# Chunked attention in a two-layer encoder: where the low half of k, the last round and five small layer-norm columns stand in the order of the work

## The chip, the cores and the metric

The program runs on one core of one Trainium2 chip. The time is the device time of one execution in microseconds; the kernel before was run three times with a median of 1211.73 us (1211.3 to 1212.54). All records of a profile come from one further execution.

## The reference, cut to what matters

Two layers act on a sequence of 512 frames with 1024 features. Layer 0 mixes with a gated linear attention, layer 1 with a softmax attention of 16 heads of 64 features in chunks of 64 frames; with eight chunks to the left, a frame sees every earlier chunk and its own. Each mixer and each squared-ReLU MLP is followed by a layer norm of `alpha*x + (1+gate)*y`, and shift, scale and gate come from a conditioning vector. The change lies in layer 1:

```
q, k, v = split(u @ w_in + b_in, 3)
s = einsum('bhtd,bhjd->bhtj', q / 8, k) + bias[h, clip(t - j)]
p = softmax(s over the keys j)
o = einsum('bhtj,bhjd->bhtd', p, v) @ w_out
x = layer_norm(alpha * x + (1 + g1) * o, ln_g, ln_b)
u = x * (1 + sc2) + sh2
```

## The kernel before, in words

Everything is held transposed: features on the 128 partitions, the 512 frames along the free dimension. A float32 product is made of three matmuls on a high and a low part of each operand (`mm3`); "hi" is a rounded copy made on ACT, "lo" the rest, made on DVE. The wrappers `V`, `A`, `G` and `T` keep each compute engine's instructions in the order in which the Python code emits them, so the order of the calls is the order of DVE, ACT, POOL and PE. (All of them carry line 47 in the profile, that of the wrapper.) DMAs are issued on SP and wait there for a free buffer.

`att` (from line 971) computes layer 1's attention in rounds `p = -1..5` (line 1091). A round makes the q and the k tile of the head pair `p + 2` and the scores of the heads `2p + 2` and `2p + 3`, and multiplies the probabilities of the heads `2p` and `2p + 1` with v:

- `mtile` multiplies one weight tile with u (24 matmuls); `evac_qk` copies the result with its bias to a tile `f` on ACT and gives back two functions: `hi` (casts of 64 rows on ACT: two for k, four for q) and `lo` (two subtractions of 64x512 on DVE). These are called `q_hi`, `q_lo`, `k_hi`, `k_lo`.
- `s_mm(h)` (line 992) makes the scores of head h, keys on partitions, in four blocks of 512, 384, 256 and 128 queries.
- `s_a(h)` (line 1006) adds the bias of each block on DVE (four `SCALAR_TENSOR_TENSOR` of ps and ng), lets ACT copy the part further than 256 from the diagonal, takes the maximum over the blocks on DVE and ends with `partition_all_reduce` on POOL, which gives the maximum over all keys, tile `mb`.
- `s_b1(h)` (line 1031) subtracts `mb` from the four blocks on DVE; `s_b2(h)` (line 1039) takes the exponential in two ACT instructions.
- `pv(h)` multiplies with v; a block of ones beside v gives the denominators. `fin1(p)` copies these on ACT and takes Ln and Exp for a first reciprocal, `fin2(p)` refines it and multiplies on DVE (four instructions), `fin3(p)` adds v's bias and splits into hi and lo.

In the rounds up to `p = 4`, DVE has the order fin2, s_b1 (odd head), fin3, s_a (even head), q_lo, s_a (odd head), s_b1 (even head), k_lo. ACT has s_b2 of the even head last, and then fin1 of the next round. The last round, `p = 5`, has an order of its own: q_hi and q_lo directly behind s_mm(12), k's evacuation ahead of s_a(12), k_lo between s_a(12) and s_a(13), and the subtraction and exponential of head 12 are left to `t1` (line 1146), which stands in the list `ev` (line 1179) of the work between attention and layer norm. There `t1`, `t2`, `t3`, `t5` finish the heads 12 to 15, mixed with the matmuls of the output projection that `boundary` makes.

`boundary` (line 330) makes the output projection, the layer norm and the next layer's input; for the attention it is called with `late=True`. Its first statement is `lnc = mk_cols()`: `ln_cols` (line 307) makes four 128x8 column constants from `ln_g`, `ln_b` and the shift and scale columns, in three `tensor_tensor` and two `tensor_scalar` on DVE. So these five stand in DVE's order directly behind the last round and ahead of `t1`. Behind `t5`, `fill` splits weights of the output projection (`wlo`, on DVE) and of the next MLP (`fhi`, `flo`).

`fill(2)` in the rounds issues the DMAs of weights until two tiles are at hand. Those of the attention's q and k and of the first four output tiles are read already split, so they cost neither DVE nor ACT anything.

Of the kernel before, what the change touches and what calls it, by code (L numbers as in the profile page):

```python
# [35 lines left out]
SH1, SC1, G1, SH2, SC2, G2 = range(6)  # L36
# [23 lines left out]
def trunk(ctx, tc, xT, c, ada, cols, gk1, gk2, w_qk, w_v, w_g, w_go, a_qk, a_v, a_tab,  # L60
# [19 lines left out]
    def bank():  # L80
        return psp.tile([P, S], F32, tag="ps", name=nm("ps"))
# [137 lines left out]
    def fill(n=None):  # L219
        n = state["look"] if n is None else n  # L220
        while len(ready_w) < n and state["pos"] < len(plan):
            emit_unit()
# [77 lines left out]
    def mtile(u, f=True):  # L300
        w = next_w(f)
        ps = bank()
        for k in range(KT):
            mm3(ps, wk(w, k), uk(u, k), k == 0, k == KT - 1)
        return ps

    def ln_cols(l, i, nxt):
        r = {}
        g = col[:, C_LNG + (l * 2 + i) * 8:C_LNG + (l * 2 + i) * 8 + 8]
        b = col[:, C_LNB + (l * 2 + i) * 8:C_LNB + (l * 2 + i) * 8 + 8]  # L310
        r["g"], r["b"] = g, b
        if nxt is not None:
            nl, sh, sc = nxt
            mS = mods[:, nl, sc * 8:sc * 8 + 8]
            mH = mods[:, nl, sh * 8:sh * 8 + 8]
            a1 = const.tile([P, 8], F32, name=nm("a1"))
            b1 = const.tile([P, 8], F32, name=nm("b1"))
            tt(V, a1, g, mS, ALU.mult)
            tt(V, b1, b, mS, ALU.mult)
            tt(V, b1, b1, mH, ALU.add)  # L320
            ag = const.tile([P, 8], F32, name=nm("ag"))
            ab = const.tile([P, 8], F32, name=nm("ab"))
            V.tensor_scalar(out=ag, in0=g, scalar1=ALPHA, scalar2=None, op0=ALU.mult)
            V.tensor_scalar(out=ab, in0=b, scalar1=ALPHA, scalar2=None, op0=ALU.mult)
            r.update(a=a1, b1=b1, ag=ag, ab=ab)
        return r
# [593 lines left out]
    def evac_qk(p, is_k, ps, h0=0, h1=S):  # L920
        hs = slice(h0, h1)
        rows = slice(0, 64), slice(64, 128)
        f = cur["tmp"].tile([P, S], F32, tag="h32", bufs=2, name=nm("f"))[:, hs]
        b, sc = (col[:, C_BK + p:C_BK + p + 1], 1.0) if is_k else (bq8[:, p:p + 1], 0.125)
        A.activation(out=f, in_=ps, func=AF.Identity, scale=sc, bias=b)
        if h0 == 0:
            (ks if is_k else qs)[p] = act_r()
            if not is_k:
                ql[p] = act_r()
                for i, r in enumerate(rows):  # L930
                    G.memset(ql[p][rows[1 - i], i, :].bitcast(F32), 0.0)
        t = (ks if is_k else qs)[p]

        def hi():
            for i, r in enumerate(rows):
                A.copy(out=t[r, i, hs], in_=f[r, :])
                if not is_k:
                    A.copy(out=t[rows[1 - i], i, hs], in_=f[r, :])

        def lo():  # L940
            for i, r in enumerate(rows):
                o = t[rows[1 - i], i, hs] if is_k else ql[p][r, i, hs]
                lo_of(V, o, f[r, :], t[r, i, hs])
        return hi, lo
# [26 lines left out]
    def att(u, es):  # L971
# [20 lines left out]
        def s_mm(h):  # L992
            p = h // 2
            q, k = qs[p], ks[p]
            pss = [bank()[:, 0:S], bank()[:, 0:384]]
            pl = bank()
            pss += [pl[:, 0:256], pl[:, 256:S]]
            for j in range(4):
                ps = pss[j]
                n = max(W[j], 256)  # L1000
                js = slice(j * P, (j + 1) * P)
                T.matmul(ps[:, 0:n], k[:, h % 2, js], q[:, h % 2, S - n:S], start=True, stop=False)
                T.matmul(ps[:, 0:n], k[:, h % 2, js], ql[p][:, h % 2, S - n:S], start=False, stop=True)
            sps[h] = pss

        def s_a(h):
            sA, sB, b = sab[h]
            sAf = sA.rearrange("p a b -> p (a b)")
            s = [sAf[:, 0:S], sAf[:, S:S + 384], sB[:, 0, 0:256], sAf[:, S + 384:2 * S]]
            for j in range(4):  # L1010
                ps = sps[h][j]
                off = max(W[j], 256) - W[j]
                nb = min(W[j], 256)
                stt(s[j][:, 0:nb], ps[:, off:off + nb], ng[:, h:h + 1], b[:, 0:nb], ALU.add, ALU.add)
                if W[j] > 256:
                    A.copy(out=s[j][:, 256:W[j]], in_=ps[:, 256:W[j]])
            mx = sB[:, 1, :]
            A.copy(out=mx[:, 0:P], in_=s[0][:, 0:P])
            tt(V, mx[:, P:S], s[0][:, P:S], s[1], ALU.max)
            tt(V, mx[:, 256:S], mx[:, 256:S], s[2], ALU.max)  # L1020
            tt(V, mx[:, 384:S], mx[:, 384:S], s[3], ALU.max)
            mb = ab_.tile([P, S], F32, tag="mb", name=nm("mb"))
            G.partition_all_reduce(mb, mx, P, bass_isa.ReduceOp.max)
            st[h] = (s, sAf)
            mbs[h] = mb
# [5 lines left out]
        def s_b1(h):  # L1031
            s, sAf = st[h]
            mb = mbs[h]
            tt(V, s[0], s[0], mb, ALU.subtract)
            tt(V, s[1], s[1], mb[:, P:S], ALU.subtract)
            tt(V, s[2], s[2], mb[:, 256:S], ALU.subtract)
            tt(V, s[3], s[3], mb[:, 384:S], ALU.subtract)

        def s_b2(h):
            s, sAf = st[h]  # L1040
            A.activation(out=sAf, in_=sAf, func=AF.Exp)
            A.activation(out=s[2], in_=s[2], func=AF.Exp)
# [10 lines left out]
        o = []  # L1053
# [37 lines left out]
        for p in range(-1, 6):  # L1091
            pq = mtile(u, False)
            s_pre(2 * p + 2)
            s_pre(2 * p + 3)
            if prev:
                fin1(*prev)
                fin2(p - 1)
            if p >= 0:
                s_b1(2 * p + 1)
            s_mm(2 * p + 2)  # L1100
            q_hi, q_lo = evac_qk(p + 2, 0, pq)
            if p == 5:
                q_hi()
                q_lo()
                fill(2)
            if prev:
                fin3(p - 1)
            if p < 5:
                s_a(2 * p + 2)
                if p >= 0:  # L1110
                    s_b2(2 * p + 1)
                fill(2)
                q_hi()
                q_lo()
                pk = mtile(u, False)
                s_mm(2 * p + 3)
                k_hi, k_lo = evac_qk(p + 2, 1, pk)
                s_a(2 * p + 3)
                k_hi()
                s_b1(2 * p + 2)  # L1120
                k_lo()
                fill(2)
                s_b2(2 * p + 2)
            else:
                pk = mtile(u, False)
                k_hi, k_lo = evac_qk(p + 2, 1, pk)
                s_b2(2 * p + 1)
                k_hi()
                s_a(2 * p + 2)
                k_lo()  # L1130
                s_mm(2 * p + 3)
                s_a(2 * p + 3)
                fill(2)
            if p >= 0:
                prev = (p, pv(2 * p), pv(2 * p + 1))
        s_pre(14)
# [8 lines left out]

        def t1():
            s_mm(14)
            s_b1(12)
            s_a(14)
            s_b2(12)  # L1150
            fill(2)
            s_b(13)

# [19 lines left out]
        def t5():  # L1173
# [3 lines left out]
            fin3(7)  # L1177

        ev = [t1, (0, range(5)), t2, (1, range(3)), e_pv(12), (1, range(3, 5)), e_pv(13), t3, (2, range(3)), t4, e_pv(14), (2, (3, 4)), e_pv(15), t5,
              (0, (5,)), (1, (5,)), (2, (5,)), (3, range(6)), (0, (6,)), (1, (6,)), (2, (6,)), (3, (6,)),  # L1180
              (0, (7,)), (1, (7,)), (2, (7,)), "shift", (3, (7,))]
# [36 lines left out]
    def opener(es, n):  # L1218
        def f():
            if es is not None:  # L1220
                es.close()
            e = ExitStack()
            cur["es"] = e
            cur["tmp"] = e.enter_context(tc.tile_pool(name=f"lnt{n}", bufs=1))
            return cur["tmp"]
        return f
# [4 lines left out]
    o, ev, es = gla()  # L1231
    evac_h, run = mlp_fns()
    u = boundary(o, 0, G1, opener(es, 0), lambda: ln_cols(0, 0, (0, SH2, SC2)), evac_h, ev)
    hs = run(u, 0)
    u = boundary(hs, 0, G2, open_v, lambda: ln_cols(0, 1, (1, SH1, SC1)), None, vfill=vfill)
    cur["es"].close()
    o, ev, es = att(u, cur["es_v"])
    evac_h, run = mlp_fns()
    u = boundary(o, 1, G1, opener(es, 1), lambda: ln_cols(1, 0, (1, SH2, SC2)), evac_h, ev, late=True)
    hs = run(u, 1)  # L1240
    boundary(hs, 1, G2, same, lambda: ln_cols(1, 1, None), None, final=True)
    cur["es"].close()
# [52 lines left out]
```

## Time and profile before

| what | value |
|---|---|
| median of 3 runs | 1211.73 us (1211.3 to 1212.54) |
| the profiled execution's own time | 1211.67 us |
| its span, first to last instruction | 1209.8 us |
| mean granted TensorE clock | 0.994 |
| busy PE / DVE / ACT / POOL | 1177.0 / 827.5 / 555.0 / 49.1 us |
| the attention's rounds and tail in the span | about 640 to 805 us |

The profiled execution stands 0.06 us below the median; 1.87 us lie outside its span. Engines: PE multiplies, DVE and ACT do the elementwise work, POOL the reductions over partitions, SP issues DMAs. A row of the timeline gives start, duration, engine, line, operation, output and input, form and count, and in brackets how long the engine had been idle before and which engine's result ended that.

### The profile page before, as it was taken

Reading aid. Unit: us, or ns where it says so; the run is one execution under the profiler, and the core shown is the slowest. Engines: PE = TensorE matmul, PEld = TensorE weight load, DVE = VectorE, ACT = ScalarE, POOL = GpSimd, SP = SyncE. Lnnn points to the kernel's source line nnn. Section 1 sums busy time; section 2 is a strip of 40 time slices with the busy share of each in tenths; the row PEclk is TensorE's granted clock in tenths of the full one; section 3 lists DMA queues with packets and bytes.
Section 4 is the critical chain, followed back from the end, with each engine's and each line's share of the span. In section 5 each row is a group of like instructions: output and inputs, shape, how many; then the busy total and the mean of one; then the engine's idle time right before and its main releaser. Section 6 shows DMA issues by size and latency. Waiting matters only on the chain.

```text
span 1209.8 us, 15107 instructions
## 1 busy us (share of the span) xinstructions
PE 1177.0 (97%) x5742; PEld 981.0 (81%) x5742; DVE 827.5 (68%) x1359; ACT 555.0 (46%) x870; POOL 49.1 (4%) x61
## 2 busy tenths in 40 slices
PE   9999999999999999999999999998999999999995
PEld 5888888888888888888888777677988888888885
DVE  6788589877676676658835878988874443443467
ACT  4565555484243342343636656564742322422324
POOL 2000000000000000000011313200000000000000
PEclk9999999999999999999999999998999999999998
DMA  9756524028889889844125340330264232332302
GB/s 347 255 184 219 186 105 161 32 88 315 306 306 339 293 305 338 297 143 157 51 104 212 123 150 34 131 115 26 68 206 144 87 105 90 103 105 87 103 2 70
DMA packets 58283, 196.34 MB, mean 162 GB/s; under 512 B 6561, under 2 KB 10913, under 8 KB 58210
## 3 DMA queue, kind: packets, MB, share of 16 engines
q1 hardware_dynamic: 58210, 195.37, 46.7%
q8 instruction: 45, 0.74, 0.2%
q14 instruction: 28, 0.23, 0.1%
HBM read 174.37 MB, written 20.97 MB: 161 GB/s over the span
## 4 chain that ended last, share of the span: by engine, by line
PE 77%; DVE 15%; ACT 6%; issue 2%; DMA 0%; DVEq 0%; ACTq 0%
PE ps L47 76%; DVE af L47 6%; DVE x L47 4%; ACT af L47 3%; ACT ar L47 1%; DVE wlo L47 1%; DVE ar L47 1%; PE warm L47 1%; ACT u L47 1%; DVE d L47 1%; DVE flo L47 1%; DVE t L47 0%; DVE y L47 0%; DVE raw L47 0%; DMA raw<-f 0%
## 5 line engine op out<-in xcount | busy, mean ns | idle before, releaser
L47 PE MATMUL ps<-ar,whi 128*128 128x512 f32 (+1 forms) x2880 | 818.4, 372 | 0.2 <-DVE ar L47 0.2
L47 PEld LDWEIGHTS ps<-ar,whi 128*128 128x128 f32 x2880 | 524.4, 189 | 95.3 <-issue 2.4
L47 PE MATMUL ps<-ar,wlo 128*128 128x512 f32 (+1 forms) x1440 | 524.8, 371 | 0.1
L47 PEld LDWEIGHTS ps<-ar,wlo 128*128 128x128 f32 x1440 | 271.8, 189 | 47.0 <-DVE wlo L47 0.8
L47 ACT CAST whi<-raw 128x1024 fp32r<-128x1024 f32 (+1 forms) x169 | 169.6, 1012 | 202.5 <-PE ps L47 156.2
L47 DVE TENSOR_TENSOR wlo<-raw,whi 128x1024 fp32r<-128x1024 f32 x162 | 197.2, 1223 | 23.3 <-ACT whi L47 21.2
L47 DVE SCALAR_TENSOR_TENSOR x<-ps,mods,x 128x512 f32<-128x512 f32 (+1 forms) x96 | 63.2, 660 | 120.2 <-PE ps L47 119.8
L47 DVE TENSOR_TENSOR h<-r 128x512 f32<-128x512 f32 (+1 forms) x72 | 45.2, 633 | 79.1 <-ACT r L47 78.2
L47 ACT ACTIVATE r<-ps 128x512 f32<-128x512 f32 (+1 forms) x72 | 39.1, 548 | 126.5 <-PE ps L47 126.5
L47 DVE SCALAR_TENSOR_TENSOR raw<-raw,csil 128x1024 f32<-128x1024 f32 x80 | 96.8, 1218 | 0.0
L47 DVE TENSOR_TENSOR ar<-h,ar 128x512 fp32r<-128x512 f32 (+1 forms) x72 | 45.6, 633 | 39.6 <-ACT ar L47 38.5
L47 PE MATMUL ps<-ar,fhi 128*128 128x256 f32 (+1 forms) x320 | 69.0, 310 | 3.7 <-DVE ar L47 2.8
L47 ACT CAST ar<-h 128x512 fp32r<-128x512 f32 (+1 forms) x72 | 41.3, 573 | 50.4 <-DVE h L47 50.4
L47 PE MATMUL ps<-whi,ar 128*128 128x512 f32 x192 | 60.7, 390 | 0.0
L47 PEld LDWEIGHTS ps<-ar,fhi 128*128 128x128 f32 x320 | 52.0, 191 | 8.1 <-DVE ar L47 4.4
L47 PE MATMUL ps<-ar,flo 128*128 128x256 f32 (+1 forms) x160 | 48.8, 305 | 0.0
L47 ACT ACTIVATE af<-x 128x256 f32<-128x256 f32 (+1 forms) x48 | 23.0, 486 | 45.4 <-DVE x L47 42.2
L47 PEld LDWEIGHTS ps<-whi,ar 128*128 128x128 f32 x192 | 36.1, 188 | 7.6
L47 ACT ACTIVATE af<-af 128x1024 f32<-128x1024 f32 (+2 forms) x48 | 32.0, 698 | 20.9 <-DVE af L47 20.4
L47 ACT CAST fhi<-raw 128x1024 fp32r<-128x1024 f32 x30 | 31.2, 1050 | 21.6 <-DMA raw<-a_qk 13.0
L47 ACT ACTIVATE ar<-x,b,a 128x256 fp32r<-128x256 f32 x48 | 28.6, 595 | 25.8 <-DVE x L47 25.8
L47 PE MATMUL ps<-af,vt 128*128 128x512 f32 (+3 forms) x128 | 36.9, 436 | 2.0 <-ACT af L47 2.0
(141 smaller groups left out, 1024.8 us busy)
## 6 DMA issues: line engine op xcount, KB each, us to landing
raw<-f SPq DMA_DIRECT2D x128, 512.0 KB, 4.4
raw<-ada SPq DMA_DIRECT2D x80, 512.0 KB, 4.7
hraw<-ada SPq DMA_DIRECT2D x16, 512.0 KB, 9.0
raw<-a_qk SPq DMA_DIRECT2D x16, 512.0 KB, 5.6
khi_q<-fhi SPq DMA_DIRECT2D x14, 512.0 KB, 3.0
klo_q<-flo SPq DMA_DIRECT2D x14, 512.0 KB, 5.3
whi<-khi_q SPq DMA_DIRECT2D x14, 512.0 KB, 3.2
wlo<-klo_q SPq DMA_DIRECT2D x14, 512.0 KB, 4.4
```

Source lines behind the costliest of these rows:

```text
L47: r = f(*a, **k)
```

## The change

Three things are reordered. No arithmetic is added or removed.

1. In the rounds up to `p = 4`, `k_lo` stands ahead of `s_b1` of the even head instead of behind it.
2. The round `p = 5` takes the order of the others, but with `k_hi` and `k_lo` ahead of `s_a(13)`. `s_b1(12)` and `s_b2(12)` move from `t1` to the end of the round.
3. `ln_cols` of the layer norm behind the attention is called ahead of `att` instead of at the start of that `boundary`.

```diff
@@ -1099,38 +1099,28 @@
                 s_b1(2 * p + 1)
             s_mm(2 * p + 2)
             q_hi, q_lo = evac_qk(p + 2, 0, pq)
-            if p == 5:
-                q_hi()
-                q_lo()
-                fill(2)
             if prev:
                 fin3(p - 1)
-            if p < 5:
-                s_a(2 * p + 2)
-                if p >= 0:
-                    s_b2(2 * p + 1)
-                fill(2)
-                q_hi()
-                q_lo()
-                pk = mtile(u, False)
-                s_mm(2 * p + 3)
-                k_hi, k_lo = evac_qk(p + 2, 1, pk)
+            s_a(2 * p + 2)
+            if p >= 0:
+                s_b2(2 * p + 1)
+            fill(2)
+            q_hi()
+            q_lo()
+            pk = mtile(u, False)
+            s_mm(2 * p + 3)
+            k_hi, k_lo = evac_qk(p + 2, 1, pk)
+            if p == 5:
+                k_hi()
+                k_lo()
+                s_a(2 * p + 3)
+            else:
                 s_a(2 * p + 3)
                 k_hi()
-                s_b1(2 * p + 2)
                 k_lo()
-                fill(2)
-                s_b2(2 * p + 2)
-            else:
-                pk = mtile(u, False)
-                k_hi, k_lo = evac_qk(p + 2, 1, pk)
-                s_b2(2 * p + 1)
-                k_hi()
-                s_a(2 * p + 2)
-                k_lo()
-                s_mm(2 * p + 3)
-                s_a(2 * p + 3)
-                fill(2)
+            s_b1(2 * p + 2)
+            fill(2)
+            s_b2(2 * p + 2)
             if p >= 0:
                 prev = (p, pv(2 * p), pv(2 * p + 1))
...
             s_mm(14)
-            s_b1(12)
             s_a(14)
-            s_b2(12)
             fill(2)
             s_b(13)
...
     cur["es"].close()
+    lnc1 = ln_cols(1, 0, (1, SH2, SC2))
     o, ev, es = att(u, cur["es_v"])
     evac_h, run = mlp_fns()
-    u = boundary(o, 1, G1, opener(es, 1), lambda: ln_cols(1, 0, (1, SH2, SC2)), evac_h, ev, late=True)
+    u = boundary(o, 1, G1, opener(es, 1), lambda: lnc1, evac_h, ev, late=True)
```

## Rows read from the trace of the kernel before

**Rows 1.** The page: span, and busy time of PE and DVE.
```profile
span 1209.8 us, 15107 instructions
...
PE 1177.0 (97%) x5742; PEld 981.0 (81%) x5742; DVE 827.5 (68%) x1359; ACT 555.0 (46%) x870; POOL 49.1 (4%) x61
```
**Rows 2.** Windows: rounds 1 and 4, last round, tail, until the statistics; columns in line one.
```profile
core 0: us, PE busy (x) PEld busy (x) DVE busy (x) ACT busy (x) POOL busy (x), PEclk, DMA share, GB/s
678.24:698.12 19.88, 19.88 (x91) 15.92 (x90) 16.44 (x31) 12.37 (x24) 4.91 (x4) 1.00 0.33 120
...
737.86:757.73 19.87, 18.41 (x82) 14.19 (x81) 16.43 (x32) 12.18 (x24) 4.90 (x4) 1.00 0.12 40
757.73:775.26 17.53, 15.43 (x68) 11.64 (x66) 16.96 (x37) 8.65 (x17) 3.95 (x2) 1.00 0.52 165
775.26:804.82 29.56, 25.95 (x106) 18.80 (x106) 26.85 (x45) 19.91 (x33) 4.11 (x2) 1.00 0.22 72
804.82:828.46 23.64, 18.05 (x133) 16.89 (x133) 20.95 (x33) 8.55 (x13) 0.00 (x0) 0.94 0.40 134
```
**Rows 3.** Timeline of DVE in round p = 4.
```profile
740.83 1.70 DVE L47 TENSOR_TENSOR af<-af,mb 128x512 f32<-128x512 f32 x4
...
746.40 2.10 DVE L47 TENSOR_TENSOR ar<-f,ar 64x512 fp32r<-64x512 f32 x2 [0.40 <-ACT ar L47]
748.52 1.53 DVE L47 SCALAR_TENSOR_TENSOR af<-ps,ng,af 128x256 f32<-128x256 f32 x4
...
751.22 2.53 DVE L47 TENSOR_TENSOR af<-af,mb 128x512 f32<-128x512 f32 x4
753.79 1.40 DVE L47 TENSOR_TENSOR ar<-f,ar 64x512 fp32r<-64x512 f32 x2
757.73 0.69 DVE L47 TENSOR_TENSOR af<-af 128x512 f32<-128x512 f32 x1 [2.54 <-ACT af L47]
```
**Rows 4.** Timeline of ACT in the same round.
```profile
748.30 0.69 ACT L47 ACTIVATE f<-ps,col 128x512 f32<-128x512 f32 x1
...
749.80 1.26 ACT L47 CAST ar<-f 64x512 fp32r<-64x512 f32 x2
753.79 1.36 ACT L47 ACTIVATE af<-af 128x1024 f32<-128x1024 f32 x2 [2.73 <-DVE af L47]
```
**Rows 5.** Who waited for whom on DVE, 674 to 800 us: total, times, longest.
```profile
DVE af L47 <- ACT af L47: 14.7, 7, 2.5
```
**Rows 6.** Timeline of POOL in the same round.
```profile
746.19 1.78 POOL L47 PARTITION_ALL_REDUCE mb<-af  x1 [11.36 <-DVE af L47]
751.47 2.08 POOL L47 PARTITION_ALL_REDUCE mb<-af  x1 [3.50 <-DVE af L47]
```
**Rows 7.** Timeline of DVE from the last round's end into the tail.
```profile
772.20 0.16 DVE L47 TENSOR_TENSOR a<-col,mods 128x8 f32<-128x8 f32 x1
...
772.47 1.04 DVE L47 TENSOR_TENSOR b<-b,mods 128x8 f32<-128x8 f32 x1
...
773.58 1.68 DVE L47 TENSOR_TENSOR af<-af,mb 128x512 f32<-128x512 f32 x4
...
776.62 1.00 DVE L47 TENSOR_TENSOR af<-af 128x384 f32<-128x384 f32 x2
...
782.32 1.02 DVE L47 TENSOR_TENSOR af<-af 128x384 f32<-128x384 f32 x2 [0.48 <-ACT af L47]
```
**Rows 8.** The chain of waits behind the tail: start, us, what.
```profile
800.66 3.51 DVE wlo L47 x3
804.18 4.23 DMA raw<-f
```
**Rows 9.** Timeline of PE at the tail's end and at the layer norm.
```profile
804.87 0.50 PE L47 MATMUL ps<-ar,fhi 128*128 128x512 f32 x1 [1.59 <-DVE ar L47]
...
828.46 2.08 PE L47 MATMUL ps<-af,ones_c 128*128 128x256 f32 x4 [5.54 <-DVE af L47]
```
**Rows 10.** Who waited for whom, 640 to 805 us: total, times, longest.
```profile
PE ps L47 <- DVE ar L47: 4.8, 4, 1.6
```

## The prediction

> **What bounds the kernel now.** I read the page first. PE is busy for 1177.0 of 1209.8 us and DVE for 827.5 [rows 1], so over the whole span PE is the bound; but the change touches the attention alone, and what it is worth must be read there.
>
> Second, the windows by round, each from one fin2 to the next. Round 1 is 19.88 us long with PE never idle; round 4 is 19.87 us long with PE idle for 1.46 [rows 2]. A round that keeps its length when PE gets idle time is not paced by PE: in the early rounds PE works off a backlog, later it waits.
>
> Third, DVE and ACT in round 4. DVE is busy without a break but for two waits: 0.40 us ahead of q_lo and 2.54 us ahead of fin2 [rows 3]. ACT waits 2.73 us for s_b1 of the even head, takes its exponential as soon as that ends (753.79), then does fin1, and fin2 starts when fin1 is done (757.73) [rows 3, 4]. That closes a loop: s_b1 ends, exponential and fin1 on ACT, fin2, s_b1 (odd), fin3, s_a, q_lo, s_a, s_b1 (even), and again. From s_b1's end (751.22 + 2.53 = 753.75) to fin2 are 3.98 us. **k_lo lies in them**: 753.79 to 755.19, while DVE could not have gone on with fin2 anyway [rows 3]. It costs the loop nothing today.
>
> Fourth, how many rounds are so. In 674 to 800 us DVE waited for ACT 7 times, 14.7 us in total, 2.5 at the longest [rows 5]. Five waits of 2.54 are 12.7; the rest are two in the tail, one of 0.48 at 782.32 [rows 7] and one of about 1.5. So the loop paces the five transitions into the rounds 1 to 5.
>
> Fifth, behind the rounds. From 775.26 to 804.82 DVE is busy for 26.85 of 29.56 us [rows 2]; PE waits at 804.87 for DVE's last fin3 [rows 9]. The chain then runs through wlo, which stands behind the last fin2 on DVE, to the load of the next MLP's weights (it needs the buffers that wlo frees) [rows 8], and PE waits 5.54 us for DVE at the statistics [rows 9]. I see no place before 828 us where a late DVE would be caught up. Afterwards PE works without such a wait, so a delay stays to the end.
>
> **The change part by part.**
>
> *k_lo ahead of s_b1.* It now lies between s_a and s_b1, on the loop, and the wait for fin1 stays whole. The price is not simply 1.40, because POOL's reduction for the odd head begins 0.25 us after s_b1 does [rows 3, 6] and stretches what DVE runs then: s_b1 takes 2.53 against 1.70 where no reduction runs, and q_lo, which has the same form as k_lo, takes 2.10 under the reduction of 746.19 against k_lo's 1.40 [rows 3, 6]. With the change the stretched one is k_lo. If s_b1 and k_lo together take as long as now in either order, s_b1 ends when k_lo does today: 755.19 - 753.75 = +1.44. By q_lo's row, 751.22 + 2.10 + 0.03 (the gap that k_lo has today) + 1.70 = 755.05: +1.30. If also a third of q_lo's 0.70 of stretch fell away, about +1.1. I take 1.4, near the first two. K_hi is done in time (749.80 + 1.26 = 751.06 [rows 4]). Five transitions: 5 x 1.4 = **+7.0**, with ends 5.5 and 7.2. The one transition before them, into round 0, has no fin1, and DVE runs on there: nothing.
>
> What it gains: PE waited 4 times for such a result of DVE, 4.8 us, of which 1.59 at 804.87 is fin3 [rows 9, 10]; the other 3.2 are waits of s_mm for k_lo. They vanish, but DVE reaches the s_a that uses those scores only after fin2 and s_b1 (odd), so this saves nothing on the loop. PE's next wait is that of s_mm and pv for free banks and exponentials, later in the same round.
>
> *The last round.* Its new order up to s_a(13) is that of round 4, except that k_hi and k_lo come ahead of s_a(13). Counted from fin2 (737.86 in round 4 [rows 2]): ACT makes `f` from 748.30 to 748.99, then k_hi, 1.26, to about 750.3 [rows 4]; the second half of k_lo follows, 0.7, to 751.0. So DVE, free for it at 748.50, waits for ACT about 1.1 us here. s_a(13) takes 751.22 - 748.52 = 2.70, to 753.75, and s_b1(12) under the reduction 2.53 [rows 3], to 756.3: 18.4 us behind fin2. Before, s_b1(12) ended at 773.58 + 1.68 = 775.26, 17.53 behind fin2 (757.73) [rows 3, 7]. That is **+0.9**. This sum already contains the gain of the third part. Bounds: -0.2 without the wait for k_hi, and +1.5 if q_hi and k_hi each keep DVE longer.
>
> *s_b2(12) ahead of s_a(14).* On ACT the exponential, 1.36 [rows 4], now stands ahead of s_a(14)'s copies, as that of head 13 stands ahead of s_a(15)'s. There DVE waits 0.48 and its first maximum begins 782.32 - 780.40 = 1.92 behind s_b1; for s_a(14) it begins 776.62 - 775.26 = 1.36 behind it, without a wait [rows 7]. **+0.55**, between 0 and 0.6. From s_b1(13) on, the order of DVE and ACT is as before.
>
> *ln_cols.* From 772.28 to 773.58 the five instructions hold DVE for 1.3 us, most of it in the third (1.04), which falls on the start of a reduction [rows 7]. With them gone the reduction stretches s_b1(12) instead (2.53 for 1.68), so the net gain is 1.3 - 0.85 = 0.45, counted above. At their new place DVE waits for PE's next tile; 0.4 us there is hidden, and 0.4 if it were not.
>
> *DMAs.* In the rounds up to 4 no load moves past another. In the last round the load of the first output tile is issued behind fin3's buffer request instead of ahead of it, and its first user is PE after s_mm(14); so 0, at most 1.
>
> **Sum**: 7.0 + 0.9 + 0.55 = +8.45 us. The span goes from 1209.8 to 1218.25, the profiled execution from 1211.67 to **1220.1**; the median of the runs shown (1211.73) lies 0.06 above it, which does not matter. By the ends, 5.5 - 0.2 = +5.3 (1217.0) and 7.2 + 1.5 + 0.6 + 1 = +10.3 (1222.0).
>
> **The rivals.**
>
> *Faster: PE paces the rounds.* If the scores' wait for k_lo set a round's length, an earlier k_lo would take away these waits, 3.2 us, and the third part its 1.3: 4.5 less, 1207.2. It decides as soon as PE's queue ends later in a round than the loop of DVE and ACT. For it: the waits stand in the trace [rows 10], and PE is 97% busy [rows 1]. Against it: DVE's own 2.54 us wait for ACT is in all five rounds [rows 5], and round 1 is as long without PE idle as round 4 with it [rows 2]. 0.06.
>
> *No change: the delay is absorbed behind the tail*, if the weights' load, not DVE, set the time of the statistics; then 1211.7. Against it: that load starts at 804.18, as the last wlo ends (800.66 + 3.51) [rows 8], and wlo is in the delayed queue. 0.05.
>
> *The reduction shuts DVE out for its whole length.* Then the second half of k_lo would begin only when the reduction ends, 751.47 + 2.08 = 753.55 [rows 6], and s_b1 would end at 753.55 + 0.7 + 0.03 + 1.70 = 755.98: +2.23 a transition, 5 x 2.23 = 11.2, with the other terms 12.6, and 1224.3 in all. Against it: under the reduction of 746.19 to 747.97 both halves of q_lo were done in 2.10 us from 746.40, while a full shut-out would end them at 747.97 + 1.4 = 749.4 instead of 748.50 [rows 3, 6]. 0.05.
> The Trainium skill states this as a rule, in "SBUF — State Buffer", section "Who interferes with whom": an operation of GpSimd, and one of VectorE with two inputs from SBUF while GpSimd's reads SBUF, exclude each other, and the second waits until the first is finished. By that rule this rival would be the forecast; the trace disagrees by 0.9 us in the q_lo above.
>
> *PE's granted clock falls in the longer gaps.* It was 1.00, the level of 2.4 GHz, in round 4 and in the last round, with 1.46 and 2.10 us of idle PE, and 0.94 in the stretch with the idle 5.54 us [rows 2, 9]. A round of about 21.3 us leaves PE some 2.9 us idle, in pieces. A third of a round at the lower level, 1.2 GHz, would cost PE 18.4 / 3 = 6.1 us, less 2.9 idle: 3.2 late, 1223.3. 0.06.
>
> **How the numbers follow.** The sum as worked out has 0.78, the four rivals 0.22. The range reaches from 1216.5, just under the lower end, to 1223.5, over the upper one and the clock's rival; the faster case, no change and the full shut-out are left out, with 0.16. A difference of about 0.2% (2.4 us) is what a measurement of this kernel tells from none. Faster 0.06; within it 0.05; slower 0.89.
>
> **What would show it.** Right: DVE's order s_a, k_lo, s_b1; rounds of about 21.3 us; DVE's wait ahead of fin2 grown from 2.54 to about 3.9; k_lo at 2.1 and s_b1 at 1.7; in the last round a wait of about 1.1 ahead of k_lo; the last fin3 about 8.4 us later than 804.82; PE's waits behind k_lo gone and others in their place. Wrong: rounds still 19.9 us long, or a wait of DVE elsewhere that shrinks as k_lo moves, or the statistics at 828 us although the tail ended later.

## The result and the profile after

The changed kernel is slower: 1221.47 us (median of 4, 1220.4 to 1221.83) against 1211.92 us, a ratio of 1.0077 (95% interval 1.0064 to 1.0089), or 9.55 us. Forecast were 1220.1 us and +8.45. Measured once more beside another set of runs of the kernel before, it stood at 1.0078 (1.0064 to 1.0091).

The windows of the changed kernel, cut at the same instructions as [rows 2] (columns in the first line):

```profile
core 0: us, PE busy (x) PEld busy (x) DVE busy (x) ACT busy (x) POOL busy (x), PEclk, DMA share, GB/s
680.30:701.61 21.31, 21.31 (x99) 17.18 (x98) 16.41 (x31) 12.26 (x24) 5.02 (x4) 1.00 0.44 159
744.21:765.51 21.30, 19.76 (x90) 15.62 (x89) 16.40 (x31) 12.21 (x24) 5.02 (x4) 1.00 0.17 59
765.51:783.97 18.46, 13.34 (x49) 9.42 (x48) 16.42 (x32) 8.57 (x17) 3.86 (x2) 0.91 0.37 132
783.97:814.00 30.03, 27.60 (x114) 19.96 (x112) 26.93 (x45) 19.78 (x33) 4.11 (x2) 1.00 0.20 71
```

A round lasts 21.30 us where it lasted 19.87, the last one 18.46 where it lasted 17.53. DVE is busy for the same time in a round (16.40 against 16.43): the new 1.43 us are all idle time of DVE. Where they lie is seen in the timeline of DVE from round 4 into the tail:

```profile
747.18 1.70 DVE L47 TENSOR_TENSOR af<-af,mb 128x512 f32<-128x512 f32 x4
...
752.74 2.10 DVE L47 TENSOR_TENSOR ar<-f,ar 64x512 fp32r<-64x512 f32 x2 [0.40 <-ACT ar L47]
...
757.68 2.13 DVE L47 TENSOR_TENSOR ar<-f,ar 64x512 fp32r<-64x512 f32 x2
759.84 1.70 DVE L47 TENSOR_TENSOR af<-af,mb 128x512 f32<-128x512 f32 x4
765.51 0.69 DVE L47 TENSOR_TENSOR af<-af 128x512 f32<-128x512 f32 x1 [3.97 <-ACT af L47]
...
777.31 1.40 DVE L47 TENSOR_TENSOR ar<-f,ar 64x512 fp32r<-64x512 f32 x2 [1.17 <-ACT ar L47]
...
781.44 2.53 DVE L47 TENSOR_TENSOR af<-af,mb 128x512 f32<-128x512 f32 x4
...
785.83 1.02 DVE L47 TENSOR_TENSOR af<-af 128x384 f32<-128x384 f32 x2 [0.42 <-ACT af L47]
```

k_lo (757.68) now stands ahead of s_b1 (759.84), and takes 2.13 us under POOL's reduction where it took 1.40 behind it; s_b1 takes 1.70 where it took 2.53 [rows 3]. DVE's wait ahead of fin2 is 3.97 where it was 2.54. The waits of the last round (1.17 ahead of k_lo) and of `t1` (0.42) are there too. On the other side of the loop, ACT waits longer for s_b1 before it can do the exponential and fin1 (timeline of ACT):

```profile
756.15 1.27 ACT L47 CAST ar<-f 64x512 fp32r<-64x512 f32 x2
761.57 1.36 ACT L47 ACTIVATE af<-af 128x1024 f32<-128x1024 f32 x2 [4.16 <-DVE af L47]
```

The 4.16 stand against 2.73 [rows 4]. DVE's waits in the whole stretch from 674 to 810 us (total, times, longest), against 14.7 us in 7 [rows 5]:

```profile
DVE af L47 <- ACT af L47: 22.2, 8, 4.0
DVE ar L47 <- ACT ar L47: 3.1, 6, 1.2
```

Of PE's three waits for k_lo before, the two in the rounds (1.12 and 1.02 us, ahead of s_mm(10) and s_mm(12)) went, and PE waits longer elsewhere: for ACT's results 8.3 us in all instead of 3.9, each time in 6 waits. PE's waits from 640 to 814 us:

```profile
PE ps L47 <- ACT af L47: 8.3, 6, 2.3
...
PE ps L47 <- DVE ar L47: 2.4, 1, 2.4
```

The third wait for k_lo, that of s_mm(14) for the last round's, did not go. It is the 2.4 in this list, and it grew from 1.02 (timeline of PE, the kernel before):

```profile
768.17 1.52 PE L47 MATMUL ps<-ar,ar 128*128 128x512 f32 x8 [1.02 <-DVE ar L47]
```

The wait for the last fin3 lies just behind this stretch: 1.53 us, against the 1.59 of [rows 10].

### The profile page after: what moved, and what is told of

It is laid out like the page before. It is cut to its first block, busy times and chain, and to the rows that moved or that the text cites. A ratio compares the mean times of both kernels' runs of the same rounds, so it can differ in the third digit from the quotient of the medians.

```text
span 1219.9 us, 15094 instructions
## 1 busy us (share of the span) xinstructions
PE 1181.1 (97%) x5742; PEld 983.0 (81%) x5742; DVE 827.3 (68%) x1359; ACT 553.7 (45%) x870; POOL 50.3 (4%) x61
## 4 chain that ended last, share of the span: by engine, by line
PE 78%; DVE 13%; ACT 6%; issue 2%; DMA 1%; SPq 0%; DVEq 0%; ACTq 0%
PE ps L47 78%; DVE af L47 4%; DVE x L47 4%; ACT af L47 3%; ACT ar L47 1%; DVE wlo L47 1%; DVE ar L47 1%; ACT u L47 1%; DMA hraw<-ada 1%; DVE d L47 1%; DVE flo L47 1%; DVE t L47 0%; DVE y L47 0%; DVE raw L47 0%; ACT L47 0%
## 5 line engine op out<-in xcount | busy, mean ns | idle before, releaser
L47 PEld LDWEIGHTS ps<-af,vt 128*128 128x128 f32 x128 | 23.8, 195 | 23.6 <-ACT af L47 9.9
L47 DVE TENSOR_TENSOR ar<-f,ar 64x512 fp32r<-64x512 f32 x32 | 31.2, 975 | 16.4 <-ACT ar L47 15.7
```

What stands on the lines that cost most here:

```text
L47: r = f(*a, **k)
```

## The experiments

Eleven kernels, and the changed one once more. Times are medians; each ratio is to the kernel before, from runs on the same chip.

| run | us | before, us | ratio (95% interval) | difference, us |
|---|---|---|---|---|
| e1: k_lo alone | 1219.63 | 1212.32 | 1.0061 (1.0049 to 1.0074) | +7.3 |
| e2: all but k_lo | 1213.41 | 1212.32 | 1.0011 (1.0002 to 1.002) | +1.1 |
| e3: ln_cols alone | 1211.17 | 1212.32 | 0.9993 (0.9984 to 1.0001) | -1.2 |
| e4: last round wholly as the others | 1219.68 | 1212.32 | 1.0063 (1.0049 to 1.0077) | +7.4 |
| e5: k_lo twice, behind | 1214.65 | 1211.94 | 1.0021 (1.0012 to 1.0031) | +2.7 |
| e6: k_lo twice, ahead | 1230.03 | 1211.94 | 1.0149 (1.0135 to 1.0163) | +18.1 |
| e7: fin1 early, kernel before | 1207.6 | 1211.94 | 0.9963 (0.995 to 0.9975) | -4.3 |
| e8: fin1 early, changed kernel | 1203.66 | 1211.94 | 0.9932 (0.9919 to 0.9944) | -8.3 |
| e9: e8 with k_lo behind | 1203.77 | 1212.48 | 0.993 (0.9918 to 0.9943) | -8.7 |
| e10: e7 with k_lo ahead | 1207.05 | 1212.48 | 0.9958 (0.9945 to 0.997) | -5.4 |
| e11: e8, last round wholly as the others | 1202.24 | 1212.48 | 0.9918 (0.9904 to 0.9931) | -10.2 |
| e12: the changed kernel again | 1221.33 | 1211.64 | 1.0078 (1.0064 to 1.0091) | +9.7 |

**e1 and e2: the change in two halves.** e1 makes the first edit in the kernel before, e2 undoes it in the changed one:

```diff
 # e1, against the kernel before, p < 5
                 k_hi()
-                s_b1(2 * p + 2)
                 k_lo()
+                s_b1(2 * p + 2)
 # e2, against the changed kernel
                 s_a(2 * p + 3)
                 k_hi()
-                k_lo()
             s_b1(2 * p + 2)
+            if p < 5:
+                k_lo()
```

> The kernel before with k_lo ahead of s_b1 in the rounds up to 4 and nothing else. Theory (k_lo leaves the wait for fin1 and goes on the loop of DVE and ACT): +7.0 us to the kernel before, between 5.5 and 7.2; rounds of 21.3 us, DVE's wait ahead of fin2 3.9 instead of 2.54. Rival (the last round's new order makes most of the loss): at most +2. Rival (PE paces the rounds): 3 faster.

> The changed kernel with k_lo back behind s_b1 in the rounds up to 4; the last round and ln_cols as changed. Theory: +1.45 us to the kernel before (0.9 in the last round, 0.55 in t1), between 0.5 and 2; rounds of 19.9 us. Rival (the last round's new order makes most of the loss): +6 or more.

k_lo alone costs 7.3 us, 0.1 above its bound; the rest costs 1.1. In e1's trace the starts of fin2 lie 21.3 us apart and DVE waits 3.97 ahead of each; in e2's they lie 19.9 apart with waits of 2.54, and s_b1(12) ends 0.89 us later than before, s_b1(13) starts 1.40 later (0.9 and 0.9 + 0.55 had been worked out). So most of the loss is that of the first edit, and the last round's order is a small rest. The halves add up to 8.4 us, about 1.2 less than the whole change; e12 looks for these.

**e3: the five small columns alone.**

```diff
+    lnc1 = ln_cols(1, 0, (1, SH2, SC2))
     o, ev, es = att(u, cur["es_v"])
...
-    u = boundary(..., lambda: ln_cols(1, 0, (1, SH2, SC2)), ..., late=True)
+    u = boundary(..., lambda: lnc1, ..., late=True)
```

> The kernel before with ln_cols ahead of the attention and nothing else. Theory: the five leave 1.3 us of DVE, and the reduction that hit them now stretches s_b1(12) by 0.85: -0.45 us, which the times can hardly tell from none; in the trace s_b1(12) takes 2.5 instead of 1.68. Rival (the whole 1.3 is gained): s_b1(12) stays at 1.7 and the tail ends 1.3 earlier.

The times leave it open whether anything is gained. The trace is clearer. The timeline of DVE in e3, s_b1(12) directly behind s_a(13):

```profile
771.93 0.29 DVE L47 TENSOR_TENSOR af<-af,af 128x128 f32<-128x128 f32 x1
772.14 2.53 DVE L47 TENSOR_TENSOR af<-af,mb 128x512 f32<-128x512 f32 x4
```

s_b1(12) takes 2.53 instead of 1.68 [rows 7]: the stretch under the reduction moved to it, as expected. It ends 0.59 us earlier than before, at 774.67, and the last fin3 is 0.60 earlier. So 0.6 of the 1.3 us are gained, and not the whole.

**e4: k_hi and k_lo behind s_a(13).**

```diff
-            if p == 5:
-                k_hi()
-                k_lo()
-                s_a(2 * p + 3)
-            else:
-                s_a(2 * p + 3)
-                k_hi()
-                k_lo()
+            s_a(2 * p + 3)
+            k_hi()
+            k_lo()
             s_b1(2 * p + 2)
```

> The changed kernel with k_hi and k_lo behind s_a(13) in the last round too, as in the other rounds. Theory: DVE's wait of 1.17 us for k_hi goes, k_lo instead of s_b1(12) is stretched by the reduction: 1.1 us less than the changed kernel, +7.2 to the kernel before. Rival (k_lo is late for s_mm(14) then and PE makes the tail later): no gain against the changed kernel.

It is 7.4 us slower than the kernel before, about 2 less than the changed kernel by the times; by the traces, less what each is late at the attention's start, s_b1(12) ends 1.1 us earlier than in the changed kernel, as worked out. PE pays for it with a longer wait for k_lo ahead of s_mm(14), which is not on the loop (timeline of PE in e4):

```profile
779.17 2.32 PE L47 MATMUL ps<-ar,ar 128*128 128x512 f32 x8 [4.14 <-DVE ar L47]
```

**e5 and e6: k_lo twice, behind s_b1 and ahead of it.** The second call writes the same values again.

```diff
 # e5, against the kernel before, p < 5
                 s_b1(2 * p + 2)
                 k_lo()
+                k_lo()
 # e6, against the changed kernel, p < 5
                 k_lo()
+                k_lo()
             s_b1(2 * p + 2)
```

> The kernel before with k_lo called twice, behind s_b1, in the rounds up to 4 (the second writes the same again). Theory (what stands behind s_b1 lies in DVE's wait for fin1): the second 1.4 us lies in the 2.54 that are left, which shrink to 1.1; 0 us, within 0.5. Rival (the sum of DVE's work paces the rounds): +7. Rival (s_mm's wait for k_lo paces the rounds): +7 too, with s_mm later by 1.4 in each.

> The changed kernel with k_lo called twice, ahead of s_b1, in the rounds up to 4. Theory: the second one costs its 1.43 us in each of five transitions, 7.1 on top of the 8.3 to 9.5 of the changed kernel: +15.5 to +16.5 to the kernel before, rounds of 22.7 us. Rival (only the first is dear, since the reduction stretches it): +9.5 or little more.

Both were off in size, e5 by 2.2 us and e6 by 1.6 past its bound. The timeline of DVE in e5 shows why:

```profile
660.84 2.84 DVE L47 TENSOR_TENSOR ar<-f,ar 64x512 fp32r<-64x512 f32 x4
663.72 1.70 DVE L47 TENSOR_TENSOR af<-af,mb 128x512 f32<-128x512 f32 x4
...
675.89 2.84 DVE L47 TENSOR_TENSOR ar<-f,ar 64x512 fp32r<-64x512 f32 x4
679.83 0.69 DVE L47 TENSOR_TENSOR af<-af 128x512 f32<-128x512 f32 x1 [1.10 <-ACT af L47]
...
768.32 1.02 DVE L47 TENSOR_TENSOR af<-af 128x384 f32<-128x384 f32 x2 [0.70 <-ACT af L47]
```

The doubled k_lo (four instructions, 2.84) cost nothing in the five transitions with a fin1: the wait ahead of fin2 shrank from 2.54 to 1.10 and the rounds stayed at 19.87. It cost its 1.4 us in the transition into round 0 (660.84), where no fin1 stands and DVE runs on without a wait, and 0.7 in the old last round, where s_mm, pk and k's evacuation came later and the copies of s_a(12) stand behind that evacuation on ACT. By the trace up to the statistics these make 2.2 of the 2.7 us. In e6 the rounds are 22.75 us long, 1.44 more than in the changed kernel; five of these and the 1.4 into round 0 make 8.6 more. That theory and rivals were told apart all the same: in the transitions with a fin1, what stands behind s_b1 is free up to the length of the wait, and what stands ahead of it is paid in full.

**e7 and e8: take the wait away.** In both kernels, fin1 of the round just ended moves ahead of s_b2 of the even head on ACT, with pv, which it needs (the edit of e8 is shown; e7 makes the same move in the kernel before):

```diff
             if prev:
-                fin1(*prev)
                 fin2(p - 1)
...
             fill(2)
+            if 0 <= p < 5:
+                prev = (p, pv(2 * p), pv(2 * p + 1))
+                fin1(*prev)
             s_b2(2 * p + 2)
-            if p >= 0:
+            if p == 5:
                 prev = (p, pv(2 * p), pv(2 * p + 1))
```

> The kernel before with fin1 ahead of s_b2 of the even head on ACT in the rounds up to 4 (pv moves with it; it is the same place for PE). Theory: fin1 then runs while ACT waits for s_b1, and fin2 follows k_lo at once: the loop loses its 2.54 us, five times, 12.7; but PE's waits of 640 to 805 us are 8.7 in all, and then PE paces: between -6 and -9 us, rounds of about 18. Rival (PE paces the rounds already): 0 to -1.

> The changed kernel with the same move of fin1. Theory: without the wait for fin1 behind s_b1 it does not matter on which side of s_b1 k_lo stands, so its 7 us vanish: within 2 us of the same move in the kernel before (what is left is the last round, up to 1.5 more), so -5 to -9 to the kernel before. Rival (k_lo ahead of s_b1 costs by itself): 7 us slower than the same move in the kernel before.

e8 lies in the range worked out, -5 to -9, but 4 us under e7 and not within 2 of it; e7 gains only 4.3 us, where at least 6 were expected. The windows of e7, rounds 3 and 4 and the last one (columns as in the section on the result):

```profile
711.94:729.75 17.81, 17.81 (x82) 14.14 (x81) 16.52 (x32) 12.10 (x24) 4.90 (x4) 1.00 0.36 132
729.75:747.55 17.80, 17.80 (x82) 14.14 (x81) 16.52 (x31) 12.05 (x24) 4.90 (x4) 1.00 0.10 36
747.55:770.79 23.24, 21.87 (x99) 17.11 (x97) 17.14 (x37) 9.85 (x19) 3.95 (x2) 1.00 0.38 132
```

and round 4 and the last round of e8:

```profile
729.15:746.96 17.81, 17.81 (x82) 14.15 (x81) 16.50 (x31) 12.06 (x24) 5.02 (x4) 1.00 0.06 17
746.96:765.73 18.77, 18.77 (x88) 15.10 (x87) 16.53 (x32) 9.84 (x19) 3.86 (x2) 1.00 0.53 182
```

In both, PE is never idle in the rounds, which are 17.8 us long: now PE paces them. But e7 gives 5.7 us back in the old last round (23.24 against 17.53). DVE waits there for ACT, in the middle of s_a(12):

```profile
761.49 1.02 DVE L47 TENSOR_TENSOR af<-af 128x384 f32<-128x384 f32 x2 [4.01 <-ACT af L47]
```

and ACT for PE's pk tile, whose evacuation stands ahead of s_a(12)'s copies in that order:

```profile
757.83 0.69 ACT L47 ACTIVATE f<-ps,col 128x512 f32<-128x512 f32 x1 [2.69 <-PE ps L47]
```

**e9 and e10: which of the two edits makes e8 better than e7?** e9 is e8 with the old place of k_lo, e10 is e7 with the new one; each edit is that of e2 or e1.

> The changed kernel with fin1 early (as in e8_fin1_early_after), and k_lo back behind s_b1 in the rounds up to 4: new last round, old place of k_lo. Theory (with fin1 early PE paces the rounds at 17.8 us and k_lo's place is worth nothing; e8 beats e7 by the last round's order alone, since in the old one s_a(12)'s copies stand on ACT behind k's evacuation, which waits for PE): as e8, 8.3 us under the kernel before, within 0.7. Rival (k_lo ahead gives PE its scores earlier and that is what e8 has over e7): as e7, 4.3 under.

> The kernel before with fin1 early (as in e7_fin1_early_before) and k_lo ahead of s_b1 in the rounds up to 4: old last round, new place of k_lo. Theory: as e7, 4.3 us under the kernel before, within 0.7, with DVE's wait of about 4 for ACT in the last round. Rival: as e8, 8.3 under.

| fin1 early | k_lo behind s_b1 | k_lo ahead of s_b1 |
|---|---|---|
| old last round | e7: -4.3 | e10: -5.4 |
| new last round | e9: -8.7 | e8: -8.3 |

e10 gained 0.4 us more than its bound. The last round's order is worth 2.9 to 4.4 us here, k_lo's place nothing that the intervals tell. In the traces, from the attention's start (DVE's first wait for q) to the statistics, the order is worth 3.9 us with either place of k_lo, and k_lo ahead 0.2 with either order. Without the early fin1 it is 7.3 and a loss. So k_lo ahead of s_b1 has no price of its own: it is dear where DVE waits for a fin1 that stands behind s_b1.

**e11: the best of these.** e8 with the edit of e4.

> The changed kernel with fin1 early and k_hi and k_lo behind s_a(13) in the last round too. Theory: the wait of 1.18 for k_hi goes, as it did without fin1 early (1.0 less): 1.0 us less than e8, 9.3 under the kernel before. Rival (PE, which waits for k_lo ahead of s_mm(14), is nearer to the bound now): no gain against e8.

1202.24 us, 0.9918 (0.9904 to 0.9931), faster than both kernels: 10.2 us under the kernel before and, by the two differences, about 20 under the changed one. Against e8 it gains 1.4 us by the times, and 0.94 at the last fin3 of the two traces; 1.0 had been worked out.

**e12: the changed kernel again.**

> The changed kernel once more, since its first measurement (9.55 us slower) is above what its own trace shows between the start and the end of the attention (8.3) and above the two halves e1 and e2 together (7.3 + 1.1 = 8.4). Theory (the 0.78 us in the first 50 us and the 0.94 in the last stores of the first profile belong to that execution, not to the change): 8.4 us slower, within 0.6, and a trace without them. Rival (they belong to the change): 9.5 again, with both in the trace.

The time came out as the first one (+9.7), so the theory on the time fell. Of the rival's two places, one was there again:

- The attention began 0.77 us late in the first profile (first wait of DVE for q at 639.42 instead of 638.65) and 0.24 in the second. That differs between executions of one kernel.
- The last store landed 2.7 us after its issue in the first profile and 2.4 in the second, against 1.7 in the kernel before. It was late in e6 too, which contains the changed order (2.5), and not in any of the ten other kernels (1.7 to 1.8). So 0.7 to 1.0 us go with the changed order. These three profiles are also the ones that end last, and no run tells the two apart; the cause is open.

From the attention's start to the statistics behind it both profiles lost 8.4 us (8.37 and 8.43), as the halves do together (e1 7.06, e2 1.42). Behind the statistics the second profile lost another 0.9, shown in the last section; this too differs between executions of one kernel. The interval (7.8 to 11) still holds the 8.4.

## Why the prediction was right, point by point

**The bound was read right.** A loop of DVE and ACT paced the rounds, and PE did not: e1 took PE's waits for k_lo out of the rounds and lost 7 us, e7 took most of the loop's wait away (0.2 us are left ahead of fin2) and the rounds fell to 17.8, in which PE is never idle.

**k_lo ahead of s_b1, +7.0.** Between the starts of fin2 of round 5, 757.73 and 765.51, lie 7.78 us, and 7.0 without the 0.77 that this execution was late before. The transition into round 0 gained 0.1, the one into round 1 cost 1.4, the four others 1.43 each; 1.4 was taken for each of the five. The stretch fell on k_lo, as q_lo's row had said: 2.13 for 2.10, and s_b1 1.70. e1 by its times: +7.3, to the statistics in its trace: +7.06.

**The last round, +0.9**: 18.46 - 17.53 = 0.93, with the wait of 1.17 ahead of k_lo for the 1.1 of the text. **s_b2(12) ahead of s_a(14), +0.55**: a wait of 0.42, and s_b1(13) starts 0.51 later. **ln_cols, a gain of 0.45** within the last round: 0.59 in e3.

**No catching up behind the tail**: the last fin3 came 8.4 us later (less the 0.77), and so did the statistics; PE's wait there was 5.52 against 5.54.

**What failed.** Not a term of the sum but what was left out of it: the measured difference is 9.6 us in two sets of runs, the sum 8.45, and the two halves, e1 and e2, also make 8.4. The forecast held the end of the program for unchanged; the last store landed 0.7 to 1.0 us later after its issue, for a reason that stays open. One reading failed as well: PE's waits of s_mm for k_lo did not all vanish. The one ahead of s_mm(14), in the last round, grew from 1.02 to 2.37 us. It cost nothing that the traces show, since DVE, not PE, sets the pace there. And the sentence on the transition into round 0, "DVE runs on there: nothing", was right for the order and would have been wrong for any work added there, as e5 shows.

**The rivals.** *PE paces the rounds* fell with e1 and e2, and came true in e7 to e11, where the wait of the loop was gone. *The delay is absorbed* fell with the statistics, which began at 837.60 instead of 828.46. *The reduction shuts DVE out* fell: in round 4 the reduction ran from 757.82 for 2.19 us, to 760.01 (timeline of POOL), while k_lo was done at 757.68 + 2.13 = 759.81 (the profile's spans of POOL are rough, but q_lo showed the same [rows 3, 6]).

```profile
757.82 2.19 POOL L47 PARTITION_ALL_REDUCE mb<-af  x1 [3.49 <-DVE af L47]
```

The Trainium skill's rule in "SBUF — State Buffer", section "Who interferes with whom", that the second of two such operations waits until the first is finished, is again stricter than the rows: k_lo grew by 0.7 us in all, and s_b1 began inside the reduction. *The granted clock falls* came true in part: it was 0.91 in the last round, but PE had idle time there, and every later term of the sum came out without it.

## What to carry to other kernels

A wait that one engine shows may be the cover of work that stands in it: before an instruction is moved ahead of another, look whether its old place lies in a wait that stays. In a loop over two in-order engines, only what stands between the wait's end and the instruction that the other engine waits for is paid; so break the wait first (here fin1 ahead of the exponential; the kernels with it gained 4 to 10 us), and the same reorderings that lost 8 to 10 us then cost nothing or gain. An order made for one bound must be tried again after the bound has changed: the old last round lost nothing under DVE's pace and 5.7 us under PE's.

## What the runs showed of the hardware that I had not expected

**TensorE's granted clock fell in the last round of the changed kernel.** PE waited 2.33 us, ran eight matmuls, and waited 2.37, the longer wait for k_lo of s_mm(14). Stretches of 2 us around the second wait (columns as in the section on the result; the third number from the end is the granted clock):

```profile
776.00:778.00 2.00, 0.00 (x0) 0.00 (x0) 0.83 (x2) 1.86 (x3) 0.00 (x0) 1.00 0.00 0
778.00:780.00 2.00, 1.93 (x9) 1.57 (x10) 1.94 (x5) 0.69 (x3) 0.00 (x0) 0.85 0.04 8
780.00:782.00 2.00, 2.00 (x6) 1.52 (x6) 1.93 (x6) 0.24 (x1) 0.31 (x1) 0.50 0.00 0
782.00:784.00 2.00, 2.00 (x9) 1.60 (x8) 2.00 (x5) 0.00 (x0) 1.76 (x1) 0.80 0.00 0
```

The lower level (0.50, or 1.2 GHz) was granted when the matmuls had already begun again. The kernel before kept 1.00 in its last round with 2.10 us of idle PE in all [rows 2].

**How soon the full clock returns behind the statistics differs between executions, by up to a microsecond of the end.** The wait there is 5.5 us in every profile. Stretches of the kernel before, of the changed kernel and of the changed kernel again, each 3.4 to 3.9 us behind the statistics' start:

```profile
832.00:834.00 2.00, 2.00 (x18) 2.00 (x17) 1.90 (x6) 0.32 (x1) 0.00 (x0) 0.92 0.00 0
```
```profile
841.00:843.00 2.00, 2.00 (x19) 2.00 (x18) 1.90 (x6) 0.42 (x2) 0.00 (x0) 1.00 0.00 0
```
```profile
841.00:843.00 2.00, 2.00 (x11) 2.00 (x11) 1.90 (x6) 0.15 (x1) 0.00 (x0) 0.50 0.00 0
```

In the third, PE made 11 matmuls in these 2 us instead of 18 or 19. Its delay against the kernel before grew by 0.92 us there (8.67 at the statistics, 9.59 behind), while that of the first profile of the same kernel went from 9.14 to 9.08. The fourteen profiles agree: the mean granted clock of the first 6 us of the statistics lies between 0.50 and 0.77, and the time from there to ACT's last instruction between 378.9 and 377.9 us, longest where the clock is lowest. So this wait is a source of spread for every kernel here.

**A tiny instruction can be as dear as a large one.** In the kernel before, a 128x8 `tensor_tensor` that starts at 772.47 took 1.04 us [rows 7], as a reduction began (timeline of POOL); in the changed kernel, at its new place without a reduction, the same one took 0.17.

```profile
772.45 1.78 POOL L47 PARTITION_ALL_REDUCE mb<-af  x1 [2.78 <-DVE b L47]
```
